# The opening of a batched matmul: a first row tile in a transfer of its own, and a fourth tile in other pieces

## Chip, cores, metric

One core of a Trainium2 chip. The metric is the time of one execution on the device in microseconds (us), the median of several. "Before" and "after" are the kernel without and with the change.

Three terms: a packet is the piece of a transfer that a DMA engine moves at a time; a count is the step by which an engine's share of a transfer, once it is done, raises the semaphore that others wait for, so the last count completes the transfer; a turn is the stretch from one packet of a queue on an engine to its next, with packets of the other queue between.

## The reference

```python
def setup_inputs():
    batch, m, k, n = 32, 512, 1024, 768
    return {"x": randn(batch, m, k) as float32, "weight": randn(batch, k, n) as float32}

def reference(x, weight):
    return np.matmul(x, weight).astype(np.float32)
```

## The kernel before

Each batch of x has four row tiles of 128 rows; partition p holds rows 4p to 4p+3. PE (TensorE, which multiplies matrices) transposes x (against `ident`), VectorE writes the transposed tile `xT` as bf16, and PE multiplies it with the weights of the batch. Weights and most of x are loaded by the pool's (GpSimd's) queue, which turns float32 into bf16 on the way. Only batch 0 is different: its x comes as float32 through the sync engine's queue, which need not wait for the pool's descriptors, and its fourth tile has a buffer of its own.

```python
    def load_w(b):
        ws[b] = w_pool.tile([P, KT, N], BF16, name="w_sb")      # w_pool: 4 buffers
        ...
            nc.gpsimd.dma_start(out=ws[b][:, at:at + n, :], in_=w_view[b, :, at:at + n, :])

    def transpose_first(mt):
        xT = xT_pool.tile([P, JT, P, 2], BF16, name="xT")
        rows = x_first[:, mt] if mt < MT - 1 else x_fourth[:, 0]
        for h in range(2):
            pt = tpsum.tile([P, JT, P], F32, name="pt")
            for i in range(JT):
                nc.tensor.transpose(pt[:, i, :], rows[:, JT * h + i::KT], ident)
            nc.vector.tensor_copy(...)
        return xT
    ...
        x_first = x_pool.tile([P, MT - 1, K], F32, name="x_sb")
        x_fourth = one_pool.tile([P, 1, K], F32, name="one_sb")
        nc.sync.dma_start(x_first, x_view[0, :, :MT - 1])
        few = [slice(at, first + 20, 4) for first in (0, 20, 40) for at in range(first, first + 4)]
        for rows in (slice(64, 96), slice(96, 112), slice(112, P), slice(60, 62), slice(62, 64), *few):
            nc.sync.dma_start(x_fourth[rows, 0], x_view[0, rows, MT - 1])
        load_w(0)
        ident = const.tile([P, P], F32)
        make_identity(nc, ident)
        load_pair(1)
        load_w(1)
        load_w(2)
        load_pair(3)
        ...
        for b in range(B):
            if b % 2 and b + AHEAD + 1 < B:
                ... load_pair(b + AHEAD + 1)
            ...
            if b + AHEAD < B:
                load_w(b + AHEAD)          # AHEAD = 3; waits for its buffer
```

(cuts marked by "...")

## Time and profile before

| | before |
|---|---|
| time | 514.59 us (514.52 to 514.70, 3 runs) |
| bytes of HBM | 218.1 MB, 425 GB/s over the span |
| DMA engines' packets | at 98% or more of the 16 engines' time from 3 to 508 us |
| PE idle | 10.3 us before its first transpose, 19.1 us before the fourth tile, 26.2 us for weights later |

PE's waits, longest first; the columns are microseconds in total, times, and the longest:

```profile
PE pm L123 <- DMA w_sb<-in_weight_dram: 26.2, 8, 4.5
PE pt L105 <- DMA one_sb<-in_x_dram: 19.1, 1, 19.1
PE pt L105 <- DMA x_sb<-in_x_dram: 10.3, 1, 10.3
```

The lower two belong to the opening, the upper one to the steady run. The pool's issues between 45 and 70 us show how much may be late; each line is the start in us, its length, the line of the program, and in brackets the wait before it:

```profile
49.52 0.53 POOL L70 DMA_DIRECT2D w_sb<-in_weight_dram  x1 [32.95 <-PE pm L123]
65.60 0.53 POOL L70 DMA_DIRECT2D w_sb<-in_weight_dram  x1 [15.55 <-PE pm L123]
```

Each of these loads waits until PE has finished a batch and so freed a weight buffer.

### The profile page before, as it was taken

How to read it: one execution, taken by the hardware profiler on the slowest of the kernel's cores; microseconds unless marked ns; L12 is line 12 of the kernel's file. 1: busy time of each engine (PE TensorE's matmuls, PEld its weight loads, DVE VectorE, ACT ScalarE, POOL GpSimd, SP SyncE). 2: the span in 40 equal slices, each digit the busy share in tenths (PEclk: the TensorE clock that was granted, in tenths of full speed). 3: DMA queues.
4: the chain of work that ended last, by engine and by line, in shares of the span. 5: the costliest groups of instructions: out<-in, count | busy, mean ns of one | idle time of the engine just before them, and what ended most of it. 6: DMA issues, size and time to landing. Idle time of an engine off the chain costs nothing.

```text
span 512.7 us, 5785 instructions
## 1 busy us (share of the span) xinstructions
PE 435.4 (85%) x2576; PEld 278.7 (54%) x2576; DVE 130.0 (25%) x196; ACT 76.1 (15%) x129; POOL 39.1 (8%) x73
## 2 busy tenths in 40 slices
PE   1806999999999996997989989798898989999991
PEld 1504666666666663654646546464464645666660
DVE  0202324141515141320413205041040410514121
ACT  1100121212121201111111111111101111120201
POOL 3000010101010101001010000101001000010000
PEclk9956999999999998997999989899798998999997
DMA  8999999999999999999999999999999999999998
GB/s 240 224 221 213 218 220 216 333 221 310 243 218 336 215 324 231 228 325 220 330 223 234 318 223 334 217 247 304 221 333 218 258 295 220 331 215 212 320 427 345
DMA packets 12712, 135.63 MB, mean 265 GB/s; under 512 B 1296, under 2 KB 1296, under 8 KB 3088
## 3 DMA queue, kind: packets, MB, share of 16 engines
q0 software_dynamic: 11440, 126.88, 96.6%
q1 hardware_dynamic: 1248, 8.39, 4.1%
q8 instruction: 20, 0.33, 0.2%
q14 instruction: 4, 0.03, 0.0%
HBM read 167.77 MB, written 50.33 MB: 425 GB/s over the span
## 4 chain that ended last, share of the span: by engine, by line
PE 46%; DMA 37%; issue 8%; DVE 5%; another core or an unknown queue 1%; POOL 1%; ACT 0%; SPq 0%; POOLq 0%
PE pm L123 40%; DMA w_sb<-in_weight_dram 28%; DMA one_sb<-in_x_dram 8%; PE pt L78 5%; DVE xT L85 4%; DVE out_sb L144 1%; POOL out_dram L164 0%; PE pt L105 0%; POOL w_sb L70 0%; POOL x_sb L60 0%; DVE one_sb L144 0%; DVE xT L93 0%; ACT out_sb L145 0%; SPq L151 0%
## 5 line engine op out<-in xcount | busy, mean ns | idle before, releaser
L123 PE MATMUL pm<-w_sb,xT 128*128 128x256 bf16 (+1 forms) x2048 | 353.7, 336 | 26.4 <-DMA w_sb<-in_weight_dram 26.2
L123 PEld LDWEIGHTS <-xT 128*128 128x128 bf16 x2048 | 205.3, 101 | 170.3 <-DMA w_sb<-in_weight_dram 29.3
L144 DVE COPY out_sb<-pm 128x512 f32<-128x512 f32 x62 | 42.9, 691 | 317.6 <-PE pm L123 317.6
L78 PE MATMUL pt<-ident,x_sb 128*128 128x128 f32 x496 | 79.8, 302 | 10.5 <-DVE xT L85 10.2
L78 PEld LDWEIGHTS pt<-ident,x_sb 128*128 128x128 f32 x496 | 69.3, 209 | 21.5 <-DVE xT L85 18.7
L85 DVE COPY xT<-pt 128x1024 bf16<-128x1024 bf16 x120 | 77.4, 687 | 11.0 <-PE pt L78 11.0
L143 ACT COPY out_sb<-pm 128x512 f32<-128x512 f32 x62 | 36.3, 585 | 271.7 <-PE pm L123 271.7
L145 ACT COPY out_sb<-pm 128x512 f32<-128x512 f32 x62 | 36.3, 585 | 145.7 <-PE pm L123 145.6
L70 POOL DMA_DIRECT2D w_sb<-in_weight_dram x37 | 20.1, 544 | 404.8 <-PE pm L123 397.6
L105 PE MATMUL pt<-ident,one_sb 128*128 128x128 f32 x8 | 1.9, 421 | 19.1 <-DMA one_sb<-in_x_dram 19.1
L106 DVE CAST xT<-pt 128x512 bf16<-128x512 f32 x8 | 5.8, 733 | 34.6 <-PE pt L105 34.1
L105 PE MATMUL pt<-ident,x_sb 128*128 128x128 f32 x24 | 5.3, 383 | 10.5 <-DMA x_sb<-in_x_dram 10.3
L105 PEld LDWEIGHTS pt<-ident,one_sb 128*128 128x128 f32 x8 | 1.6, 219 | 19.4 <-issue 19.4
L164 POOL DMA_DIRECT2D out_dram<-out_sb x14 | 10.1, 719 | 6.7 <-ACT out_sb L143 3.5
L105 PEld LDWEIGHTS pt<-ident,x_sb 128*128 128x128 f32 x24 | 4.1, 209 | 11.5 <-issue 10.3
L60 POOL DMA_DIRECT2D x_sb<-in_x_dram x15 | 8.1, 539 | 10.9 <-DMA w_sb<-in_weight_dram 10.9
L144 DVE COPY one_sb<-pm 128x512 f32<-128x512 f32 x2 | 1.4, 690 | 9.0 <-PE pm L123 9.0
L93 DVE COPY xT<-pt 128x1024 bf16<-128x1024 bf16 x4 | 2.6, 686 | 0.2 <-PE pt L78 0.2
L143 ACT COPY one_sb<-pm 128x512 f32<-128x512 f32 x2 | 1.2, 585 | 6.4 <-PE pm L123 6.4
L145 ACT COPY one_sb<-pm 128x512 f32<-128x512 f32 x2 | 1.2, 585 | 1.6 <-PE pm L123 1.6
L143 ACT ACT_TABLE_LOAD x1 | 1.3, 1283 | 0.7 <-PEq L232 0.7
L64 POOL DMA_DIRECT2D x_sb<-in_x_dram x1 | 0.5, 528 | 2.1 <-DMA w_sb<-in_weight_dram 2.1
(6 smaller groups left out, 0.9 us busy)
## 6 DMA issues: line engine op xcount, KB each, us to landing
w_sb<-in_weight_dram POOLq DMA_DIRECT2D x28, 1536.0 KB, 41.7
out_dram<-out_sb POOLq DMA_DIRECT2D x14, 3072.0 KB, 55.3
x_sb<-in_x_dram POOLq DMA_DIRECT2D x15, 2048.0 KB, 49.8
w_sb<-in_weight_dram POOLq DMA_DIRECT2D x7, 768.0 KB, 38.2
out_dram<-out_sb SPq DMA_DIRECT2D x2, 1536.0 KB
x_sb<-in_x_dram SPq DMA_DIRECT2D x1, 1536.0 KB
out_dram<-one_sb SPq DMA_DIRECT2D x2, 768.0 KB
out_dram<-out_sb SPq DMA_DIRECT2D x2, 768.0 KB
```

The source lines that it names most:

```text
L60: nc.gpsimd.dma_start(out=xs[b], in_=pair_view[b // 2])
L70: nc.gpsimd.dma_start(out=ws[b][:, at:at + n, :], in_=w_view[b, :, at:at + n, :])
L78: nc.tensor.transpose(pt[:, j, :], pairs[:, mo, j::JT], ident)
L85: nc.vector.tensor_copy(both[:, :, :, :, half, :].rearrange("p b j i r -> p j b i r"), words(b, mt + MT * half).rearrange("p j (b i r) -> ...
L93: nc.vector.tensor_copy(xT.rearrange("p j m r -> p (j m r)"), words(B - 1, mt).rearrange("p j m -> p (j m)"))
L105: nc.tensor.transpose(pt[:, i, :], rows[:, JT * h + i::KT], ident)
L106: nc.vector.tensor_copy(xT[:, 2 * h:2 * h + 2].rearrange("p j m r -> p j r m"), pt.rearrange("p (j r) m -> p j r m", r=2),)
L123: nc.tensor.matmul(pm[bank][:, at:at + size], xT[:, ko // 2, :, ko % 2], ws[b][:, ko, off:off + size], start=(ko == 0 and not (together an ...
L143: nc.scalar.copy(o[:, 0:512], pm[0])
L144: nc.vector.tensor_copy(o[:, 512:1024], pm[1])
L145: nc.scalar.copy(o[:, 1024:N2], pm[2])
L164: nc.gpsimd.dma_start(out=two_view[at], in_=twos[at])
```

## The change

Its intent: let PE start on the first tile long before the three are there, and deal the fourth tile's rows out over the DMA engines in other portions (13 transfers of five rows, none of two).

```diff
-        nc.sync.dma_start(x_first, x_view[0, :, :MT - 1])
+        for tiles in (slice(0, 1), slice(1, MT - 1)):
+            nc.sync.dma_start(x_first[:, tiles], x_view[0, :, tiles])
         few = [slice(at, first + 20, 4) for first in (0, 20, 40) for at in range(first, first + 4)]
-        for rows in (slice(64, 96), slice(96, 112), slice(112, P), slice(60, 62), slice(62, 64), *few):
+        for rows in (slice(80, 112), slice(112, P), slice(65, 80), slice(60, 65), *few):
             nc.sync.dma_start(x_fourth[rows, 0], x_view[0, rows, MT - 1])
```

## The prediction

> **What bounds the kernel now.** I read the page first, then the table of busy time by stretches, the timeline of the opening, the chain that ended last in order of time, and the trace's own DMA packets and semaphore counts. The page says what is full:
>
> ```profile
> PE   1806999999999996997989989798898989999991
> ...
> DMA  8999999999999999999999999999999999999998
> ...
> q0 software_dynamic: 11440, 126.88, 96.6%
> q1 hardware_dynamic: 1248, 8.39, 4.1%
> ...
> HBM read 167.77 MB, written 50.33 MB: 425 GB/s over the span
> ```
>
> The DMA row is at 9 from the second slice to the last but one; PE has a hole in the third slice (about 25.6 to 38.5 us) and shallow ones later. 167.77 + 50.33 = 218.1 MB over 512.7 us is the 425 GB/s. I then added up the packet times of the trace in steps of 1 us: the 16 engines are at 0.98 or more of their time in every step from 3 to 508 us, none excepted. So nothing that PE waits for in the opening lets the DMA engines run dry. The stretches say the same:
>
> ```profile
> 24.00:42.90 18.90, 0.00 (x0) 0.03 (x1) 0.00 (x0) 0.33 (x1) 0.00 (x0) 0.60 1.03 222
> ...
> 197.40:423.60 226.20, 195.23 (x1122) 122.18 (x1120) 56.12 (x85) 33.37 (x57) 17.80 (x31) 0.93 1.02 265
> 423.60:502.00 78.40, 76.54 (x464) 49.00 (x464) 20.86 (x32) 13.57 (x24) 4.61 (x8) 0.98 1.02 293
> ```
>
> The column before last is the DMA share, the first after the length PE's busy time. In 24 to 42.9 PE does nothing at all while DMA is at 1.03 (a sum of overlapping packets, so it can pass 1). From 197.4 to 423.6 PE is idle 226.2 - 195.2 = 31 us, and the waits of PE put 26.2 us in 8 waits on weights. The chain shows where PE last catches up with the transfers:
>
> ```profile
> 373.89 49.68 DMA w_sb<-in_weight_dram
> 423.57 0.05 issue
> 423.62 12.05 PE pm L123 x63
> ```
>
> After that PE has all its input in time until its last matmul at 501.8, and the stores that were held back keep the DMA engines busy until their last count at 511.7. The end is therefore set by bytes through the engines; PE's lateness after the opening is made good by 197 us, where it begins to wait for weights again.
>
> **The opening.** These are the lines that the change touches:
>
> ```profile
> 0.74 0.38 SPq L151 DMA_DIRECT2D x_sb<-in_x_dram  x1
> 1.18 27.82 SPq L154 DMA_DIRECT2D one_sb<-in_x_dram  x17
> ...
> 10.34 5.41 PE L105 MATMUL pt<-ident,x_sb 128*128 128x128 f32 x24 [10.34 <-DMA x_sb<-in_x_dram]
> ...
> 15.86 7.96 PE L123 MATMUL pm<-w_sb,xT 128*128 128x512 bf16 x48
> ...
> 42.90 1.94 PE L105 MATMUL pt<-ident,one_sb 128*128 128x128 f32 x8 [19.08 <-DMA one_sb<-in_x_dram]
> ```
>
> PE waits 10.34 us for the one transfer of three row tiles, transposes them, multiplies from 15.86, runs out of rows at 23.82 and waits 19.08 us for the fourth tile. The first wait looks like what the change removes. But the semaphore counts of the trace show the first weights complete at 15.82 and the three tiles at 10.20: the first matmul starts 0.04 us after the weights landed. Its two conditions (the first transposed tiles, the weights) are met together, and making one earlier leaves the other.
>
> **What the Trainium skill says, and whether the trace agrees.** "DMA: Bandwidth & Descriptors", section "Queues, rings and completion order", has each engine alternate between the queues that have work, one packet at a time. The trace agrees: after the pool's first packet (6.0 us) the small row packets stand 1.98 us apart beside weights (packet 0.925 us, twice, plus 0.172 for the 4 KB row) and 2.57 us beside pairs of x (1.226 us, twice, plus 0.172). So a small transfer costs an engine two turns, one for the row, one for its count. The section "Why a DMA increments its semaphore by 16 and not by 1" of that page says that a transfer from this queue uses the largest number of engines up to 16 that divides its rows, the lowest-numbered ones: 5 rows five engines, 2 rows two, 15 rows fifteen. The packets agree: groups of five, and two engines that lag (counts of the last five-row transfer at 39.38 to 39.48 on three engines, at 42.66 and 42.71 on two). "Issuing engines are not separate DMA queues" there: all queues share the same 16 engines; agreed, the shares add up to 1. "TensorE: Matmul & The Clock Gate", section "What's actually happening": an idle PE falls to half clock after about 3.4 us. The granted clock 0.60 in 24 to 42.9 agrees.
>
> **The change, part by part.** The bytes are the same: the first three tiles as 128 x 12 KB before, 128 x 4 KB plus 128 x 8 KB after, and 128 rows of the fourth tile either way. Issues on the queue: 1 + 17 = 18 before, 2 + 16 = 18 after.
>
> First tile alone. The queue's first packet was at 1.76 us and the pool's at 6.0, so the first 8 packets of 4 KB an engine run nearly alone: about 0.7 us for the start and 8 x 0.17 us, landed at about 4 to 4.5 us instead of 10.20. PE transposes tile 0 from there. Gain on the path: none, since the weights land near 15.8.
>
> Tiles 1 and 2. Before, 109 of the 128 packets had started by 6.0 us, so 13 engines had one packet left and three two. Small packets are a little slower: 0.172 us for 4 KB is 23.8 GB/s, 0.46 us for 12 KB is 26.7; for 96 KB an engine I estimate 8 x (0.172 + 0.31) = 3.86 instead of 8 x 0.46 = 3.68 us, +0.18. About one and a half 8 KB packets are then left at 6.0, so up to one more turn (0.93 us): landing at 9.5 to 11.5. The 16 transposes at 5.41/24 = 0.23 us each take about 3.7 us and end by 15.2; still no later than the weights.
>
> Fourth tile. Engines 0 and 1 before: 12 five-row and 2 two-row transfers, 14 small ones; engines 2 to 4 twelve. After: 13 on all five. The large ones take 4 rows and 3 counts an engine in both (the 15 rows leave engine 15 out). One small transfer less on the two engines that came last: the last but one landed there at 41.31, so the end moves from 42.71 to 41.3. The extra turn of tiles 1 and 2, if it comes, gives back 0.9. I put the fourth tile at 41.8, 0.9 earlier, and the wait before it still at about 18 us.
>
> DMA work by engine, which sets the end. Rows of 4 KB in this tile: engines 0 and 1 18 before, 17 after; 2 to 4 16 before, 17 after; others 4 in both, engine 15 3. A row and its count cost 0.172 + 0.022 = 0.19 us. These five engines are the late ones of every weight transfer: the 128-row transfer that landed at 51.13 counted on eleven engines by 49.29 and on five only at 50.90 to 51.13, and near the end the spread is still 2.7 us (509.09 to 511.74). So the last engine gets -0.19 (if it is 0 or 1) or +0.19 (if 2 to 4), and +0.18 + 0.02 from the split of the first three tiles. Sum: 0.0 to +0.4 us, centre +0.1 to +0.2. Nothing else that the DMA engines do changes. 514.59 + 0.1 = 514.7.
>
> **The rivals.**
> 1. PE's start is on the path: then 0.9 us earlier gives 513.7. For it: the chain runs through the fourth tile and from it straight to the next stage. Against it: PE waits for weights 26.2 us after 197 us, and a chain over PE only passes on what the DMA engines, full in every microsecond, don't take back. If the whole 10 us before the first transpose were on the path, and the fourth tile were as much earlier, it would be about 505; the fourth tile can't be, its 13 small transfers still go behind 26 large packets.
> 2. The fourth tile comes later, because the first three take more turns, and the engines run dry. Batch 0 then ends later, and the load into its weight buffer is issued later than 49.52, the next later than 65.60. The trace shows transfers landing at 68.09 and 75.38, the fastest engine done at 72.96, so the issue at 65.60 has some 5 us to spare, less its own start (4.7 us from first issue to first packet in the opening, an upper estimate as it held other work). Two to three turns too many, 2 to 3 us, would cost at most about 1 to 2 us: 516. I give this one in twenty.
> 3. Even loads on engines 0 to 4 help: the end then falls by up to 0.2 us plus what the count packets waste, 514.3. For it the two lagging engines; against it that the split adds about as much to all.
> 4. An idle gap between tile 0 and tile 1 (4 us or so) lets PE fall to half clock, and the 16 transposes take up to 3.7 us more, past 15.8. It would be lost in the 19 us hole: 0 on the time.
>
> **Range and chances.** The runs of before lie within 0.18 us of each other. The sum's own uncertainty is about 0.3, and another chip or day adds some tenths. 514.1 to 515.4 should hold it eight times in ten. 2% is 10.3 us; a gain needs fewer bytes or idle DMA time to fill, and there is less than 3 us of the latter at the two ends. A loss of 2% needs the engines idle for 10 us. Faster 0.01, same 0.98, slower 0.01.
>
> **What would show it.** Right: PE's first transpose near 4 to 5 us; its first matmul still within 0.5 us of 15.8 and right after the first weights' last count; PE idle from about 24 to 41 or 43; DMA at 9 in all slices but the ends; the last counts of the fourth tile close together on five engines; waits for weights of some 27 us after about 195. Wrong: first matmul well before 15; a slice or microsecond of DMA below 0.95 around 65 to 80 us; an end moved by more than 1 us with DMA full, which would mean that bytes per second, not idle time, changed.

## The result

514.86 us (514.73 to 515.34, 6 runs) against 514.64 (514.44 to 515.07, 6 runs): ratio 1.0005, 95% interval 0.9992 to 1.0018, the same. Ratios here and below are the mean time of one kernel's fast runs over that of the other's of the same rounds, so not quite the ratio of the medians that stand beside them.

The timeline of the opening, after:

```profile
5.37 1.95 PE L105 MATMUL pt<-ident,x_sb 128*128 128x128 f32 x8 [5.37 <-DMA x_sb<-in_x_dram]
...
11.35 3.89 PE L105 MATMUL pt<-ident,x_sb 128*128 128x128 f32 x16 [4.03 <-DMA x_sb<-in_x_dram]
...
15.69 7.96 PE L123 MATMUL pm<-w_sb,xT 128*128 128x512 bf16 x47 [0.46 <-DMA w_sb<-in_weight_dram]
...
41.96 1.94 PE L105 MATMUL pt<-ident,one_sb 128*128 128x128 f32 x8 [18.31 <-DMA one_sb<-in_x_dram]
```

The first transpose starts at 5.37 instead of 10.34 us, but the first matmul at 15.69 instead of 15.86: it now waits for the weights in plain sight, and the trace has them complete at 15.65. The fourth tile's wait is 18.31 instead of 19.08 us, its transposes 0.94 us earlier. What PE won it waits for later; its waits, after:

```profile
PE pm L123 <- DMA w_sb<-in_weight_dram: 30.0, 10, 4.9
PE pt L105 <- DMA one_sb<-in_x_dram: 18.3, 1, 18.3
...
PE pt L105 <- DMA x_sb<-in_x_dram: 9.4, 2, 5.4
```

The waits for weights grew by 3.8 us, more than the 1.7 us that the two others shrank. Part of that may be the record: 48 of the 2048 matmuls are missing from this profile, and in a second one of the same kernel with none missing (`h3_after` below) the growth is 2.3 us (28.5) and the others shrank by 1.9. The page's DMA row differs only in its last digit, 7 instead of 8:

```profile
DMA  8999999999999999999999999999999999999997
...
q0 software_dynamic: 11440, 126.88, 96.6%
q1 hardware_dynamic: 1392, 8.39, 4.1%
```

The first number is packets: 144 more on the sync engine's queue (128 for the split tiles, 16 for their counts), the same megabytes. The last counts of the final stores run from 508.81 to 512.24 us over the 16 engines (before: 509.09 to 511.74). The mean of the 16 moved by 0.11 us (510.72 to 510.83), the last of them by 0.50. Which of them is last decides the end.

### The profile page after: what moved, and what is told of

Its sections match the earlier page's. It is cut to its first block, busy times and chain, and to the rows that moved or that the text cites. A ratio compares the mean times of both kernels' runs of the same rounds, so it can differ in the third digit from the quotient of the medians.

```text
span 513.2 us, 5738 instructions
## 1 busy us (share of the span) xinstructions
PE 432.0 (84%) x2528; PEld 278.7 (54%) x2576; DVE 130.0 (25%) x196; ACT 76.1 (15%) x129; POOL 39.1 (8%) x73
## 4 chain that ended last, share of the span: by engine, by line
PE 46%; DMA 37%; issue 8%; DVE 5%; another core or an unknown queue 1%; POOL 1%; ACT 0%; SPq 0%; POOLq 0%
PE pm L123 40%; DMA w_sb<-in_weight_dram 29%; DMA one_sb<-in_x_dram 6%; PE pt L78 5%; DVE xT L85 4%; DMA x_sb<-in_x_dram 2%; DVE out_sb L144 1%; POOL out_dram L165 0%; PE pt L105 0%; POOL x_sb L60 0%; POOL w_sb L70 0%; DVE one_sb L144 0%; DVE xT L93 0%; ACT out_sb L145 0%
## 5 line engine op out<-in xcount | busy, mean ns | idle before, releaser
L123 PE MATMUL pm<-w_sb,xT 128*128 128x256 bf16 (+1 forms) x2000 | 349.7, 334 | 32.5 <-DMA w_sb<-in_weight_dram 30.0
## 6 DMA issues: line engine op xcount, KB each, us to landing
w_sb<-in_weight_dram POOLq DMA_DIRECT2D x28, 1536.0 KB, 41.8
```

Source lines behind the costliest of these rows:

```text
L123: nc.tensor.matmul(pm[bank][:, at:at + size], xT[:, ko // 2, :, ko % 2], ws[b][:, ko, off:off + size], start=(ko == 0 and not (together an ...
```

## The experiments

Twelve kernels, all correct. The theory at the start: the DMA engines are full, so neither PE's start nor the fourth tile's arrival is on the path, up to some microseconds of lateness. The rival: PE's start is on the path.

The trace does not name the engine of a packet or of a count, but each 128-row transfer leaves 16 counts (a five-row transfer leaves five), which I take for one from each engine that took part. For each kernel I took the 16 counts of the very last store and their distances from their own mean. This table, worked out from those counts, goes with all that follows (us; "time" is the ratio to before of the same rounds):

```
kernel             fourth tile  waits for  mean of the  last of   time
                   on PE at     weights    16 counts    them
before                 42.90      26.2       510.72     511.74
after                  41.96      30.0       510.83     512.24    1.0005
h3_after               41.93      28.5       510.90     512.13    1.0006
e1_split_only          44.23      27.1       511.08     512.54    1.0016
e2_rows_only           41.54      27.5       510.99     512.16    1.0004
e3_even16              26.68      40.2       511.50     513.95    1.0032
e4_one_transfer        23.52      42.4       510.87     514.20    1.0038
f1_eights              40.42      29.9       510.40     513.34    1.0015
f2_eights_half         33.87      35.8       510.69     513.37    1.0016
h1_sixes               41.40      29.8       510.67     513.27    1.0024
i1_split_four          41.82      27.7       510.88     512.02    0.9998
g1_pe_later5           42.96      25.2       510.93     512.19    0.9997
g2_pe_later12          42.91      26.2       512.57     516.10    1.0077
h2_pe_later16          42.88      27.4       523.69     526.80    1.0297
```

The counts are those of one profiled execution each. For e1, e4, f1 and f2 it was the slowest of the five, for before the fastest of its rounds (514.44 us), so the differences of the counts overstate those of the time.

### The two parts alone

Edits: one of the two hunks of the change each.

> Only the first three tiles are split, the fourth tile's transfers are those of before. Theory (the DMA engines are full, bytes decide): first transpose near 5.3 us as in the changed kernel, first matmul within 0.3 us of 15.7 because the weights land there, fourth tile at 43 to 44 us (one turn more for engines 0 and 1 than before), time +0.0 to +0.4 us against before. Rival (PE's start is on the path): the fourth tile later by 1 us makes it +1 us.

Measured: 515.50 us against 514.56, ratio 1.0016 (1.0003 to 1.0029). First transpose at 5.41, first matmul at 16.06 just after the weights (16.02), fourth tile at 44.23 (its last count at 43.92, one turn later, as expected). The time is above the expected 0.4 us.

> Only the fourth tile's transfers are changed, the first three tiles come in one transfer. Theory: first transpose at 10.3 us as before, fourth tile near 41 us (one small transfer less on the last two engines), time -0.2 to +0.2 us against before. Rival (PE's start is on the path): -1 to -1.5 us.

Measured: 514.90 us, ratio 1.0004 (0.9992 to 1.0017). Fourth tile at 41.54. 1.4 us earlier on PE bought nothing, which speaks against the rival.

### The fourth tile much earlier

```diff
-        for rows in (slice(64, 96), slice(96, 112), slice(112, P), slice(60, 62), slice(62, 64), *few):
+        for rows in [slice(at, at + 16) for at in range(0, P, 16)]:      # e3_even16
+        for rows in (slice(0, P),):                                      # e4_one_transfer
```

> The fourth tile in 8 transfers of 16 rows, one row an engine each, instead of 17 of which 12 go to five engines. 8 x 2 = 16 turns instead of 35 before it lands: near 24 to 27 us, so that PE's hole of 19 us shrinks to about 1 to 3 us. Theory: the time moves only by the more even load of the engines, -0.8 to +0.2 us; waits of PE for weights grow by about as much as the hole shrank, to 40 us and more. Rival (PE's start is on the path): -15 us or so.

> The fourth tile in one transfer of 128 rows, right behind the first three: 8 rows and one count an engine, 9 turns: near 18 to 21 us, before PE has used up the first three tiles (23.8) or just then; the hole is gone. Theory: time -0.8 to +0.2 us as for the eight transfers; the waits for weights take up the 19 us. Rival (PE's start is on the path): -19 us. A third possibility, that PE early makes buffers free early and so changes nothing but the order in which the transfers are asked for, is the same as the theory in time.

Measured: 516.35 us, ratio 1.0032 (1.0018 to 1.0045), and 516.62 us, 1.0038 (1.0026 to 1.0051). PE's waits in the run with 8 x 16 rows:

```profile
PE pm L123 <- DMA w_sb<-in_weight_dram: 40.2, 13, 4.5
PE pt L105 <- DMA x_sb<-in_x_dram: 10.3, 1, 10.3
...
PE pt L105 <- DMA one_sb<-in_x_dram: 2.4, 1, 2.4
```

and the timeline of the run with one transfer:

```profile
15.73 7.96 PE L123 MATMUL pm<-w_sb,xT 128*128 128x512 bf16 x48
23.52 1.05 PE L105 MATMUL pt<-ident,one_sb 128*128 128x128 f32 x8
24.96 2.77 PE L123 MATMUL pm<-w_sb,xT 128*128 128x256 bf16 x16 [0.38 <-DVE xT L106]
```

The hole of 19 us is gone (2.4 us, and none at all), the waits for weights rose from 26.2 to 40.2 and 42.4, and the kernel did not become faster. The rival, which stood for -15 and -19 us, has fallen. But both are slower by 1.8 and 2.1 us, where my theory had 0 or a small gain, so something else in these pieces matters. The counts show what: in the 8 x 16 run the third pool transfer's 16 counts lie within -0.24 and +0.30 us of their mean; the one that lands at 417 us has eight engines at -1.82 to -0.68 and eight at +1.01 to +1.68; the last store eight at -1.69 to -1.15 and eight at +0.86 to +2.44. With the same bytes on every engine one half falls behind steadily: the eight late counts come 0.30 us after the eight early ones, mean against mean, at 33 us, 0.63 at 92, 2.88 at 417, and 3.05 at the end, 0.6% of 511 us (with one transfer: 0.47 at 34, 2.94 at 418). The idea that follows is that the many five-row transfers of before are a counterweight: they load five engines with 12 to 14 rows more than the rest. It does not explain everything: of the 2.21 us by which the last count moved in the 8 x 16 run, 0.78 are in the mean of the 16, which moving load between engines should not shift. That part stays open.

### Is it a counterweight, and on which engines?

The edits, each in place of the same line of before (h1's list is written out here):

```diff
+        for rows in [slice(at, at + 8) for at in range(0, P, 8)]:        # f1_eights
+        for rows in [slice(at, at + 16) for at in range(64, P, 16)] + [slice(at, at + 8) for at in range(0, 64, 8)]:   # f2_eights_half
+        for rows in (slice(80, 112), slice(112, P), slice(78, 80), *[slice(at, at + 6) for at in range(0, 78, 6)]):    # h1_sixes
```

> The fourth tile in 16 transfers of 8 rows. New theory, from the run with 8 x 16 rows (last counts of eight engines 1.2 to 1.7 us before the mean of the 16, of the other eight 0.9 to 2.4 after it): half of the engines are slower over the run by some 3 us, the fast half are the lowest eight, and the fourth tile's transfers act as a counterweight that loads fast engines. 8 rows go to the lowest eight engines, 16 rows each there and none on the others, 16 x 0.19 = 3.1 us. If so: spread of the last counts below 2 us (before: 2.65), the three engines that end 1.2 to 1.6 us early before are gone, time -0.2 to -1.0 us against before. If the fast half are other engines, the spread grows beyond 4 us and the time by 1 us and more. Theory of bytes alone without engines: 0. Fourth tile lands near 39 to 41 us in either case.

> Half the dose: 4 transfers of 16 rows and 8 of 8 rows, 12 rows on the lowest eight engines and 4 on the others, a counterweight of 1.5 us instead of 3.1. Counterweight theory: between the even 8 x 16 rows (+1.7 us) and the 16 x 8 rows: +0.3 to +1.0 us against before, spread 2.5 to 3.5 us. Theory of bytes alone: 0. PE start theory: the fourth tile lands near 33 us, 10 us earlier, so -10 us, already against the runs.

Measured: 515.65 us, ratio 1.0015 (1.0003 to 1.0028), and 515.81 us, 1.0016 (1.0003 to 1.0030). Neither of my two guesses was right as stated: the spread of the last counts with 8-row transfers is 5.9 us, not below 2, and yet the time is no worse than with even rows (the intervals overlap). The counts fit this reading: two engines at -2.95 and -2.83, eight from -0.72 to -0.11, four from +0.70 to +1.06, two at +2.82 and +2.94. Against the 8 x 16 run the lowest eight engines carry 8 rows more and the others 8 fewer, 8 x 0.19 = 1.5 us up and down. Added to the two halves of that run, slow engines that are loaded land at +2.4 to +3.9, and fast ones that are not at -3.2 to -2.7: there are two of each. So six of the lowest eight would be fast and two slow. This assignment is inferred, not read from the trace, and it supposes that the same engines are slow on each chip, which was not tested. The half dose would load the same two slow engines (it has two at +2.36 and +2.68), so it could not beat before either. PE's start is no rival here: the fourth tile reaches PE at 40.42 us with 8-row transfers, and at 41.40 in the next run, about as late as after the change (41.96), and both are slower.

> The counterweight on six engines: 13 transfers of six rows, one of 2, one of 32 and one of 16, no split of the first tiles. From the runs with 16 x 16 turns and 8-row transfers, of the lowest eight engines six are fast and two slow, and the five that the kernel before loads are fast. If the sixth engine is fast too: the engines that end early fall from three to two, spread 2 to 3 us, time -0.3 to +0.3 us against before. If it is one of the slow two: one engine ends 2 to 3.5 us after the mean, time +1.5 to +2.5 us. If the counterweight is not the cause of the 1.8 us that even rows lost: 0 in either case.

Measured: 515.96 us, ratio 1.0024 (1.0011 to 1.0037), the case "one of the slow two", though its time fell below the +1.5 to +2.5 us that I expected for it: fifteen engines end between -1.79 and +0.97 us, a single one at +2.60. Adding one engine to the counterweight adds one late engine. That is a clear sign, not a reading, that the five-row transfers fit five fast engines; a sixth costs 0.0024 x 514.6 = 1.2 us.

### How late may PE be?

The transfers stay as before; PE repeats the four transposes of the fourth tile's first half, with the same result.

```diff
             pt = tpsum.tile([P, JT, P], F32, name="pt")
-            for i in range(JT):
-                nc.tensor.transpose(pt[:, i, :], rows[:, JT * h + i::KT], ident)
+            for _ in range(7 if mt == MT - 1 and h == 0 else 1):     # 17 in g2, 41 in h2
+                for i in range(JT):
+                    nc.tensor.transpose(pt[:, i, :], rows[:, JT * h + i::KT], ident)
```

> PE does the four transposes of the first half of the fourth tile seven times instead of once (same result, same transfers): batch 0 ends about 5 to 6 us later. Theory (slack, the engines have work until about 72 us): the two loads into freed weight buffers are issued near 55 and 71 instead of 49.5 and 65.6, time 0 to +1.0 us. Rival (PE's start is on the path): +5 to +6 us.

> The same seventeen times: batch 0 ends 12 to 14 us later, the second of those loads is issued near 78 to 79 us, when the engines have had nothing to do since about 72 to 75. Theory: a hole of 4 to 8 us in the DMA engines between 72 and 81 us, and the time longer by as much as the hole, +4 to +8 us, with PE's waits for weights shorter by 5 to 9 us. Theory without any slack limit (DMA never matters): 0. PE start on the path: +12 to +14.

> The four transposes of the fourth tile's first half forty-one times, 0.10 us each as measured with seventeen times (6.4 us): batch 0 ends some 16 us later, the loads into freed buffers are issued near 65.5 and 81.6 instead of 49.5 and 65.6. The engines have work until 66 to 68 us and, after the first of the two, until about 75. Slack theory: a first hole of 0 to 2 us near 67, a second of 6 to 8 us from about 75, the time +8 to +13 us (the dried-up engines and one that restarts late, which cost 4.1 us with 6.4 us of lateness). If lateness only costs once through one engine that restarts late: +4 to +5 us.

The repeats were shorter than I had reckoned: the load at 49.52 us was issued at 51.45, 55.91 and 67.26, so the doses are 1.9, 6.4 and 17.7 us (my labels promise other ones).

1.9 us: 514.73 us, ratio 0.9997 (0.9984 to 1.0011). Free.

6.4 us: 518.77 us, ratio 1.0077 (1.0063 to 1.0091), +4.1 us. The pool's issues of this run:

```profile
55.91 0.53 POOL L70 DMA_DIRECT2D w_sb<-in_weight_dram  x1 [39.30 <-PE pm L124]
71.98 0.53 POOL L70 DMA_DIRECT2D w_sb<-in_weight_dram  x1 [15.54 <-PE pm L124]
```

The second load comes at 71.98, when the fastest engine is just done (72.96 was its last count before). I expected a hole of 4 to 8 us; the summed packet times show only 0.25 us of idle at 72 to 75 us. The cost is elsewhere: of the packets that start from 70 to 78 us, ten took over 1.5 us, where before all took at most 0.93, the counts of the tenth pool transfer are 2.0 us later in the mean, and one engine is 2.7 us after the mean of the 16 and 2.2 after the next. It stays behind to the end (+3.53; the next +2.30).

17.7 us: 529.57 us, ratio 1.0297 (1.0280 to 1.0315), +15.0 us, above my 8 to 13, as the dose was above the intended 16. By stretches (start:end and length, then the busy time of PE, its weight loads, VectorE, ScalarE and the pool, then granted clock, DMA share, GB/s):

```profile
60.00:70.00 10.00, 9.12 (x69) 7.58 (x69) 4.30 (x7) 0.58 (x1) 0.53 (x1) 1.00 0.76 148
...
75.00:80.00 5.00, 5.00 (x33) 3.05 (x32) 0.69 (x1) 1.17 (x2) 0.00 (x0) 1.00 0.27 57
80.00:85.00 5.00, 5.00 (x33) 2.99 (x31) 0.69 (x1) 1.17 (x2) 1.67 (x3) 1.00 0.26 29
```

Here the roles are reversed: PE is busy and the engines are dry, in two places, at 65 to 69 and 76 to 84 us, together 10.3 us by the summed packet times. The mean of the last counts moved by 13.0 us (the 10.3, and 2.7 more, which I put down to slow restarts: the tenth pool transfer is already 13.0 later in the mean), the last of them by 15.1, because the spread grew by 2.1. PE's waits for weights stayed at 27.4 us: what the engines lose comes back nowhere.

This run also tests the counterweight, without being meant to. Before it ran dry, its late eight counts stood 1.50 us after the early eight at 68 us, as in before (1.41). The dry time wiped that out: 0.35 us at 94 us. From there the distance grows as with even rows, to 2.44 at 414 us. In before, which kept the lead that the five-row transfers had made, it falls, from 1.67 at 124 us to 0.93 at 416. The rate is about the same: 2.1 us in 320 here, 2.25 in 325 with even rows. So the uneven loads of the opening do hold the end together; which engines they are stays inferred.

### The changed kernel again, and the split with other rows

> The changed kernel itself again, beside before on the same chip, because the split alone measured +0.9 us and the rows alone +0.2 to +0.3: if the two parts add up, +0.9 to +1.2 us; as in its first measurement, +0.1 to +0.5 us. The counterweight theory says +0.1 to +0.5: the split by itself slows the start a little, the rows take the two latest engines' extra transfer away.

Measured: 514.86 us against 514.59, ratio 1.0006 (0.9993 to 1.0018), as the first time. The parts do not add up to more.

```diff
+        for tiles in (slice(0, 1), slice(1, MT - 1)):
+            nc.sync.dma_start(x_first[:, tiles], x_view[0, :, tiles])
-        ... slice(60, 62), slice(62, 64), *few):
+        ... slice(60, 64), *few):                                        # i1_split_four
```

> The split as in the changed kernel, the fourth tile as before except that its two transfers of 2 rows are one of 4 rows (engines 0 to 3 one row each): 13 small transfers on engines 0 to 3, 12 on the fifth, where split alone had 14 on two engines. It asks whether split alone (+0.9 us) was slower than the changed kernel (+0.2 to +0.3) because two engines had one small transfer more. If so: +0.0 to +0.4 us, last counts no later than 512.3. If the split costs 0.9 us wherever it is and the changed kernel's rows gave it back in another way (the 15-row transfer leaves the last engine out): +0.7 to +1.0 us. Fourth tile lands near 41 to 42 us.

Measured: 514.85 us against 514.79, ratio 0.9998 (0.9984 to 1.0011), last count at 512.02. So the split as such costs nothing that these rounds can see. That the split alone measured +0.9 us fits its extra small transfer on two engines (its last count is at 512.54), but its interval overlaps that of the changed kernel, and the same two transfers of 2 rows cost nothing visible in before; this stays open.

No variant beat before: the table's best, 0.9997 and 0.9998, are equal to it within their intervals.

## Why the prediction was right, point by point

**The bound.** "The end is set by bytes through the engines." Shown from both sides: PE 16 to 19 us earlier at the fourth tile gave no gain, and the DMA engines idle for 10.3 us cost all of it and more (+15.0).

**First tile.** Predicted to land at 4 to 4.5 us, PE from there; the last count was at 5.23 and the transpose at 5.37. The 128 packets of 4 KB ran from 1.77 us to 3.63 on the engine that was through first and to 4.88 at the latest. Half of them took no more than 0.174 us, near the 0.172 that I took from packets further on, but some up to 0.93, and the mean was 0.25: the term 8 x 0.17 was too small. The sum had a second fault that hid this: 1.76 + 0.7 + 8 x 0.17 is 3.8, not 4 to 4.5, and where its 0.7 us for the start comes from is not said. No effect, as the weights' last count (15.65) gated the first matmul (15.69), as predicted.

**Tiles 1 and 2.** Predicted at 9.5 to 11.5, came at 11.21. The remainder at the pool's first packet was 45 packets of 8 KB, 2.8 an engine, instead of my one and a half, for the same reason. The transposes ended before the weights were there.

**Fourth tile.** Predicted at 41.8 us with counts close together on five engines. The counts of the last five-row transfer are at 41.33 to 41.73; before, three engines had theirs by 39.48 and two at 42.66 and later. (The turns that the prediction reads, 1.98 and 2.57 us, are 0.04 and 0.05 less than its own sums of packets, 2.02 and 2.62.)

**Size.** Predicted +0.1, measured +0.2 to +0.3, inside the range and not distinguishable from 0. That nothing would change was understood; that the +0.1 came so near shows nothing, since the noise is as large, and counts as luck, since the sum behind it seems to have the wrong engines late. The last counts moved by 0.50, the means by 0.11. The step "these five engines are the late ones of every weight transfer" holds for the opening (51.13 us) but seems to fail for the end: I read the spread of 2.7 us at 511.74 as the same five. The even rows showed that half of the engines fall behind by 0.6%; that the five are not among these, and that loading them keeps the end together, is what the runs with eights and sixes and the dry run indicate. (The idle DMA time at the two ends, "less than 3 us", is 4.3 by the packets, 1.8 of it before the first one; nothing rests on it.) Rival 3, even loads on the five, was tried by the rows alone: ratio 1.0004, no gain. The wider form, which I expected of the 8 x 16 rows, had the wrong sign: even loads over all 16 cost 1.8 us.

**Rivals 1 and 2.** Rival 1 fell. Rival 2's threshold, "some 5 us to spare, less its own start", fits the runs: 1.9 us late was free, 6.4 us cost 4.1. Its way of reckoning the price was too low, since it counted only idle time, and 0.25 us of that came with a loss of 4.1.

**Rival 4.** The gap between tile 0 and tile 1 was 4.03 us after. It could not let PE fall to half clock, for PE was there already: eight transposes took 1.95 us at 5.37 us, as at 41.96 (1.94), where the trace records half clock, against 1.05 at full clock in the run with one transfer. The trace's first clock record is of full clock and begins at 15.23 us (before: 14.05); where there is no record, the views print 1.00. In the profiles of the split alone and of the split with a four-row transfer it begins only at 20.24 and 20.01 us, and the 48 matmuls after the first three tiles took 10.00 and 9.84 us instead of 7.96: in the first of these, 15 matmuls from 16 to 20 us and 27 from 20 to 24. Why the full clock came later there was not tested, and the loss went into the wait for the fourth tile.

## What to carry to other kernels

Before making an input earlier, look whether the engine that waits for it waits again, later, for something that is already running without a break: then the early wait is only moved. Ask instead how late the waiting engine may be before the running one has nothing queued, and measure that with dummy work. And where transfers fill all the time, compare the 16 counts of the last transfer: small transfers that use few engines, even in the opening, can decide which engine ends last.

## What the Trainium skill lacked or had wrong

- "DMA: Bandwidth & Descriptors", section "Latency and other measured facts", names engines 7 and 15 as usually slower. Here, with equal rows, eight of the 16 fell behind the other eight by 3.05 us in 511 (0.6%). The trace doesn't say which; the runs with 8-row and six-row transfers suggest that two of the lowest eight are among them.
- The same page, section "Specifications", has about 1 us to the first byte for the pool's transfers. The first one here was issued at 1.26 us and its first packet was at 5.98 (4.7 us), with other work of the pool in between.
- No page has the price of a restart after the queues ran dry: with 0.25 us of idle the counts came 2.0 us later in the mean, ten packets took over 1.5 us instead of 0.93 at most, and one engine stayed 2.7 us behind the mean; with 10.3 us idle another 2.7 us were lost in the mean.
- No page has it that the first 128 packets of 4 KB, before any of the pool's, took 0.25 us in the mean and up to 0.93 (median 0.174), where those from 12 to 45 us took 0.17.
